# The MLP's two products as seven products of halves, with weight sums made by accumulating transfers

## The chip, the cores and the metric

One core of a Trainium2 chip runs the whole program. The time is device microseconds of one execution; lower is better. TensorE (PE) multiplies, VectorE (DVE), ScalarE (ACT) and GpSimd (POOL) work on tiles of 128 partitions in the on-chip memory SBUF, TensorE's sums lie in PSUM, and 16 DMA engines carry data between DRAM and SBUF. SyncE (SP) and POOL each have a queue that issues transfers; each engine works through its own instructions in order.

## The reference

One decoder layer in float32, 512 tokens of 2048 features: attention of 16 heads, then the part that is changed here.

```python
h = h + mix                                   # after the attention's output projection
h = h + squared_relu_mlp(rms_norm(h, norm_mlp_g[i]), mlp_w_in[i], mlp_w_out[i])

def squared_relu_mlp(h, w_in, w_out):         # w_in 2048 x 8192, w_out 8192 x 2048
    return jnp.square(jax.nn.relu(h @ w_in)) @ w_out
```

## The kernel before

Everything is held transposed: features on the partitions, the 512 tokens on the free axis. A float32 product is made of three: each operand is split into two float32r parts, `hi` (a rounded copy, made by ACT) and `lo` (the rest, made by DVE or POOL), and hi*hi + hi*lo + lo*hi go through TensorE into one PSUM bank. A weight block is 128 x 1024 (512 KB); SP loads it into `raw`, ACT casts it to `whi` (L101), DVE subtracts for `wlo` (L102). Each of these three names has 4 buffers.

The projections of q, k and v and the attention come first (L364 to L377) with heads staged between projection steps; then the output projection (`quad` on `wo`, L386 to L413). Its results are added to x into `y` (L419), and `hh`, `hl`, the two parts of y times the gain, and the sum of squares `acc2` (POOL, L430) are made on the way.

The MLP runs in 16 chunks of 512 hidden features. `mlp_in` multiplies a chunk of `w1` with `hh` and `hl` over 8 blocks (L140 to L142: weights stationary, 512 tokens moving); the token's RMS factor `rstd2` is made inside chunk 0 (L438 to L442) and applied to the products (L447), so that nothing waits for it. ACT squares and casts, DVE makes the rest (L449 to L451). `mlp_out` multiplies the chunk before with 8 blocks of `w2` (L463 to L465) and adds every bank into `y` (L467). The last chunk's sums are stored at once (L469). The order on each engine is set by a scheduler that follows the program's order and the buffers.

## Time and profile before

| | |
|---|---|
| runs | 2239.5 and 2240.43 us, median 2239.97 |
| profiled execution: span | 2237.2 us |
| instructions | 23734, of which 9866 matmuls and as many weight loads |
| PE / PEld / DVE / ACT / POOL busy | 99% / 82% / 47% / 32% / 13% |
| granted TensorE clock | full in every slice |
| moved by DMA | 215.46 MB, 96 GB/s over the span |

Of the profiled execution the span is given, from its first instruction to its last; the launch that surrounds it is only in the runs' times. A view of lines gives for each group of instructions the busy time, the mean of one, the idle time of its engine just before, and what ended most of that. PEld is the loading of the stationary side, shown as an engine of its own. Matmuls are pipelined, so one is shown as lasting longer than the distance between two starts.

### The profile page before, as it was taken

How to read it: one execution, taken by the hardware profiler on the slowest of the kernel's cores; microseconds unless marked ns; L12 is line 12 of the kernel's file. 1: busy time of each engine (PE TensorE's matmuls, PEld its weight loads, DVE VectorE, ACT ScalarE, POOL GpSimd, SP SyncE). 2: the span in 40 equal slices, each digit the busy share in tenths (PEclk: the TensorE clock that was granted, in tenths of full speed). 3: DMA queues.
4: the chain of work that ended last, by engine and by line, in shares of the span. 5: the costliest groups of instructions: out<-in, count | busy, mean ns of one | idle time of the engine just before them, and what ended most of it. 6: DMA issues, size and time to landing. Idle time of an engine off the chain costs nothing.

```text
span 2237.2 us, 23734 instructions
## 1 busy us (share of the span) xinstructions
PE 2213.0 (99%) x9866; PEld 1830.6 (82%) x9866; DVE 1053.6 (47%) x1178; ACT 723.8 (32%) x846; POOL 294.4 (13%) x150
## 2 busy tenths in 40 slices
PE   8999999999999999999999999999999999999999
PEld 7878878878888888888888888888888888888887
DVE  6574573673685334434334334344343343343343
ACT  5454454454464223212222222212222122222221
POOL 5444434434411111000000000000000000000000
PEclk9999999999999999999999999999999999999999
DMA  6222222222223333233332232332232323323323
GB/s 216 85 67 76 85 76 76 85 66 84 79 74 104 113 118 117 85 104 96 100 96 94 94 104 88 101 104 94 96 102 86 104 95 102 96 94 94 104 86 112
DMA packets 60443, 215.46 MB, mean 96 GB/s; under 512 B 6832, under 2 KB 6832, under 8 KB 60336
## 3 DMA queue, kind: packets, MB, share of 16 engines
q1 hardware_dynamic: 60336, 213.95, 29.8%
q8 instruction: 77, 1.26, 0.2%
q14 instruction: 30, 0.25, 0.0%
HBM read 209.73 MB, written 4.19 MB: 96 GB/s over the span
## 4 chain that ended last, share of the span: by engine, by line
PE 87%; DVE 8%; ACT 3%; POOL 1%; issue 1%; DMA 0%; SPq 0%; POOLq 0%; ACTq 0%; DVEq 0%
PE pm L141 13%; PE pm L140 13%; PE pm L142 13%; PE po L463 10%; PE po L465 10%; PE po L464 10%; PE pq L254 2%; PE pq L252 2%; PE pq L253 2%; PE pv L221 2%; PE pv L223 2%; PE pv L222 2%; DVE nb L115 1%; DVE sp L307 1%; DVE sp L304 1%
## 5 line engine op out<-in xcount | busy, mean ns | idle before, releaser
L101 ACT CAST whi<-raw 128x1024 fp32r<-128x1024 f32 (+1 forms) x385 | 405.2, 1052 | 1166.5 <-PE pm L141 566.0
L102 DVE TENSOR_TENSOR wlo<-raw,whi 128x1024 fp32r<-128x1024 f32 (+1 forms) x297 | 371.7, 1252 | 628.0 <-ACT whi L101 626.4
L140 PE MATMUL pm<-hh,whi 128*128 128x512 f32 x1024 | 398.7, 389 | 0.0
L142 PE MATMUL pm<-hh,wlo 128*128 128x512 f32 x1024 | 398.4, 389 | 0.0
L141 PE MATMUL pm<-hl,whi 128*128 128x512 f32 x1024 | 398.4, 389 | 0.0
L463 PE MATMUL po<-u,whi 128*128 128x512 f32 x1024 | 398.3, 389 | 0.0
L464 PE MATMUL po<-u,whi 128*128 128x512 f32 x1024 | 398.3, 389 | 0.0
L465 PE MATMUL po<-u,wlo 128*128 128x512 f32 x1024 | 398.3, 389 | 0.0
L467 DVE TENSOR_TENSOR y<-po,y 128x512 f32<-128x512 f32 x256 | 176.5, 689 | 248.4 <-PE po L465 247.7
L102 POOL TENSOR_TENSOR wlo<-raw,whi 128x1024 fp32r<-128x1024 f32 x88 | 224.3, 2549 | 303.0 <-ACT whi L101 303.0
L141 PEld LDWEIGHTS pm<-hl,whi 128*128 128x128 f32 x1024 | 192.3, 188 | 40.1 <-issue 0.2
L140 PEld LDWEIGHTS pm<-hh,whi 128*128 128x128 f32 x1024 | 192.3, 188 | 40.0 <-issue 0.2
L465 PEld LDWEIGHTS po<-u,wlo 128*128 128x128 f32 x1024 | 192.3, 188 | 39.9
L142 PEld LDWEIGHTS pm<-hh,wlo 128*128 128x128 f32 x1024 | 192.3, 188 | 39.9
L464 PEld LDWEIGHTS po<-u,whi 128*128 128x128 f32 x1024 | 192.3, 188 | 39.9
L463 PEld LDWEIGHTS po<-u,whi 128*128 128x128 f32 x1024 | 192.3, 188 | 39.8
L252 PE MATMUL pq<-xh,whi 128*128 128x512 f32 x512 | 200.1, 391 | 0.0
L254 PE MATMUL pq<-xh,wlo 128*128 128x512 f32 x512 | 199.4, 390 | 0.0
L253 PE MATMUL pq<-xl,whi 128*128 128x512 f32 x512 | 199.3, 389 | 0.0
L252 PEld LDWEIGHTS pq<-xh,whi 128*128 128x128 f32 x512 | 96.1, 188 | 20.5 <-ACT whi L101 0.2
L253 PEld LDWEIGHTS pq<-xl,whi 128*128 128x128 f32 x512 | 96.1, 188 | 20.5 <-issue 0.2
L254 PEld LDWEIGHTS pq<-xh,wlo 128*128 128x128 f32 x512 | 96.1, 188 | 20.4
(151 smaller groups left out, 2178.3 us busy)
## 6 DMA issues: line engine op xcount, KB each, us to landing
raw<-w SPq DMA_DIRECT2D x256, 512.0 KB, 3.5
raw<-wqk SPq DMA_DIRECT2D x64, 512.0 KB, 3.5
raw<-wo SPq DMA_DIRECT2D x32, 512.0 KB, 3.4
raw<-wv SPq DMA_DIRECT2D x31, 512.0 KB, 3.5
raw<-xT SPq DMA_DIRECT2D x15, 512.0 KB, 3.9
out<-y SPq DMA_DIRECT2D x16, 256.0 KB, 2.0
raw<-xT SPq DMA_DIRECT2D x2, 256.0 KB, 3.7
raw<-wv SPq DMA_DIRECT2D x2, 256.0 KB, 4.6
```

The lines of the kernel that those rows point to most:

```text
L101: nc.scalar.copy(hi, raw)
L102: lo_engine.tensor_tensor(lo, raw, hi.bitcast(F32), op=ALU.subtract)
L140: nc.tensor.matmul(pm[m], wh[:, ww], ah[k], start=k == 0, stop=False)
L141: nc.tensor.matmul(pm[m], wh[:, ww], al[k], start=False, stop=False)
L142: nc.tensor.matmul(pm[m], wl[:, ww], ah[k], start=False, stop=k == 2 * nb - 1)
L252: nc.tensor.matmul(pq, wh[:, ww], xh[k], start=k == 0, stop=False)
L253: nc.tensor.matmul(pq, wh[:, ww], xl[k], start=False, stop=False)
L254: nc.tensor.matmul(pq, wl[:, ww], xh[k], start=False, stop=k == KC - 1)
L463: nc.tensor.matmul(pm, wh[:, ww], uh[k], start=k == 0, stop=False)
L464: nc.tensor.matmul(pm, wh[:, ww], ul[k], start=False, stop=False)
L465: nc.tensor.matmul(pm, wl[:, ww], uh[k], start=False, stop=k == 3)
L467: nc.vector.tensor_tensor(ym, pm, ym, op=ALU.add)
```

## The change

The matrices of both MLP products are cut in halves in each direction, and each product of 2 x 2 halves is made by seven products instead of eight (one level of Strassen's scheme). With x11 to x22 the quarters of the left side and w11 to w22 those of the weights, products 1, 5, 6 and 4 take the weights w11, w11 + w12, w11 + w12 + w22 and w11 + w12 + w22 + w21 (signs lie on the other operand or in the adds), product 3 takes w22, 7 takes w12 + w22, 2 takes w21. They run in the order 1, 5, 6, 3, 7, 2, 4. The sums of weights are made by DMAs that POOL issues with `accum_op=ALU.add`: `plus` adds a block from DRAM onto a block in SBUF. w11 becomes in turn the four sums, in the same buffers.

The first product now runs in 16 units (`g`), each 7 products of 48 matmuls with 256 tokens moving; the second in 16 units (`s`, `fp`), each 7 products of 24 matmuls, with the hidden activations stationary and 512 output features moving, so that its result has tokens on the partitions. `y` is therefore transposed on TensorE after the output projection and written to DRAM (`yd`), and read back as `z` before the second product. The RMS factor is made before the first product and applied to `y` (`norm`), from which `make` forms the seven left operands in unit 0. The hidden activations' seven operands, in two parts, are written to DRAM for each unit of the first product (`put`: 14 pieces of 256 KB, POOL's queue) and read for each unit of the second (`fetch`, SP's queue). The part of the program up to the output projection is as it was, but for the pools that some constants come from.

```diff
-                nc.scalar.activation(hh[m], ym, AF.Copy, scale=g_sb[:, 1, m:m + 1])
-                nc.vector.scalar_tensor_tensor(
-                    hl[m], ym, g_sb[:, 1, m:m + 1], hh[m].bitcast(F32),
-                    op0=ALU.mult, op1=ALU.subtract,
-                )
...
+    pr = bank("pr")
+    nc.tensor.matmul(pr, ones_d, acc2, start=True, stop=True)
+    rstd2 = st("rstd2")
+    newton_rstd(st("r0"), st("nb"), pr, rstd2)
+    nc.vector.tensor_scalar(rstd2, rstd2, -0.5, None, op0=ALU.mult)
+    yd = dram.tile([P, KC * S], F32, name="yd")
+    def quarter(th, fp, fh):
+        return slice(((th * 2 + fp) * 2 + fh) * 1024, ((th * 2 + fp) * 2 + fh + 1) * 1024)
+    for c4 in range(4):
+        for t in range(4):
+            pt = pb.tile([P, S], F32, name="pt", tag="pb")
+            for i in range(4):
+                nc.tensor.transpose(
+                    pt[:, i * P:(i + 1) * P], y[:, 4 * c4 + i, t * P:(t + 1) * P], ident
+                )
+            ys = st("ys")
+            nc.scalar.copy(ys, pt)
+            q = quarter(t // 2, c4 // 2, c4 % 2).start + (t % 2) * S
+            nc.gpsimd.dma_start(yd[:, q:q + S], ys)
...
+    pp = ctx.enter_context(tc.tile_pool(name="pp", bufs=4, space=PSUM))
+    def banks(name):
+        return pp.tile([P, 1024], F32, name=name, tag="pp")
+    def operand(r, i, part):
+        name = f"x{r}{part}{i}"
+        if r in (1, 2, 4):
+            return mp.tile([P, S], F32R, name=name, tag=name)
+        k = 4 * {5: 0, 6: 1, 7: 2, 3: 3}[r] + i
+        return big.tile([P, S], F32R, name=name, tag=f"a{part}{k}")
+    def products(src):
+        def chunk(i, j, pool, tag):
+            ts = [pool.tile([P, 1024], F32, name=tag, tag=tag, bufs=4) for _ in range(2)]
+            for c in range(2):
+                nc.sync.dma_start(ts[c], src[i, j, c])
+            return ts
+        def plus(ts, i, j):
+            for c in range(2):
+                nc.gpsimd.dma_start(ts[c], src[i, j, c], accum_op=ALU.add)
+        w11 = chunk(0, 0, wpool, "raw")
+        w22 = chunk(1, 1, mp, "mraw")
+        w12 = chunk(0, 1, mp, "mraw")
+        plus(w12, 1, 1)
+        w21 = chunk(1, 0, wpool, "raw")
+        into = {1: w11, 5: w11, 6: w11, 4: w11, 3: w22, 7: w12, 2: w21}
+        then = {1: (0, 1), 5: (1, 1), 6: (1, 0)}
+        for r in ORDER:
+            parts = []
+            for c in range(2):
+                w = into[r][c]
+                hi, lo = wtile("whi"), wtile("wlo")
+                split_w(hi, lo, w, nc.vector)
+                parts.append((hi, lo))
+            if r in then:
+                plus(w11, *then[r])
+            yield r, parts
...
+    def split(r, i, src):
+        hi, lo = operand(r, i, "hi"), operand(r, i, "lo")
+        nc.scalar.copy(hi.rearrange("p (o c) -> p o c", o=2), src)
+        nc.vector.tensor_tensor(
+            lo.rearrange("p (o c) -> p o c", o=2), src,
+            hi.rearrange("p (o c) -> p o c", o=2).bitcast(F32), op=ALU.subtract,
+        )
+        xs[r, i] = hi, lo
+    def block(t, k, i):
+        return y[:, 8 * k + 2 * i:8 * k + 2 * i + 2, 256 * t:256 * (t + 1)]
+    def norm(k):
+        for c in range(8 * k, 8 * k + 8):
+            nc.vector.scalar_tensor_tensor(
+                y[:, c, :], y[:, c, :], g_sb[:, 1, c:c + 1], rstd2, op0=ALU.mult, op1=ALU.mult
+            )
+    def make(r):
+        tt = nc.vector.tensor_tensor
+        if r == 1:
+            norm(0)
+        for i in range(4):
+            x11, x12, x21, x22 = (block(t, k, i) for t in range(2) for k in range(2))
+            if r == 1:
+                split(1, i, x11)
+            elif r == 5:
+                split(4, i, x22)
+                tt(x22, x21, x22, op=ALU.subtract)
+                split(5, i, x22)
+            elif r == 6:
+                tt(x21, x11, x21, op=ALU.subtract)
+                tt(x11, x22, x11, op=ALU.subtract)
+                split(6, i, x11)
+            elif r == 3:
+                split(2, i, x12)
+                tt(x12, x12, x11, op=ALU.add)
+                split(3, i, x12)
+            elif r == 7:
+                split(7, i, x21)
+    ud = [dram.tile([P, 14 * S], F32R, name=f"ud{g}") for g in range(NG)]
+    for g in range(NG):
+        ps, kept = {}, {}
+        for r, parts in products(w1[g]):
+            if g == 0:
+                make(r)
+            b = {1: "A", 2: "A", 6: "B", 7: "B", 4: "B", 5: "C", 3: "C"}[r]
+            new = b not in ps
+            if new:
+                ps[b] = banks(f"p{b}")[:, :S]
+            for c, (wh, wl) in enumerate(parts):
+                for kk in range(4):
+                    k = 4 * c + kk
+                    h, l = (x[:, (k % 2) * 256:(k % 2 + 1) * 256] for x in xs[r, k // 2])
+                    for m in range(2):
+                        ww = slice(kk * 256 + m * P, kk * 256 + (m + 1) * P)
+                        o = ps[b][:, m * 256:(m + 1) * 256]
+                        kw = dict(stop=False, skip_group_check=True)
+                        nc.tensor.matmul(o, wh[:, ww], h, start=new and k == 0 and m == 0, **kw)
+                        nc.tensor.matmul(o, wh[:, ww], l, start=False, **kw)
+                        nc.tensor.matmul(o, wl[:, ww], h, start=False, stop=k == 7,
+                                         skip_group_check=True)
+            tt = nc.vector.tensor_tensor
+            if r == 1:
+                p1 = kept[2, 1] = st("p1")
+                nc.scalar.copy(p1, ps["A"])
+            elif r == 5:
+                q = kept[2, 2] = st("q")
+                tt(q, ps["C"], p1, op=ALU.subtract)
+            elif r == 6:
...
+            elif r == 2:
+                u = kept[1, 1] = st("u")
+                nc.scalar.activation(u, ps["A"], AF.Relu)
+                nc.scalar.activation(u, u, AF.Square)
+            else:
+                tt(p1, ps["B"], p1, op=ALU.add)
+            if r in (3, 7, 4):
+                u = {3: v, 7: q, 4: p1}[r]
+                nc.scalar.activation(u, u, AF.Relu)
+                nc.scalar.activation(u, u, AF.Square)
+        if spill is None:
+            spill = big.tile([P, KC, S], F32R, name="spill", tag="acc")
+        def put(r, u):
+            hi, lo = spill[:, r - 1, :], spill[:, 7 + r - 1, :]
+            nc.scalar.copy(hi, u)
+            nc.vector.tensor_tensor(lo, u, hi.bitcast(F32), op=ALU.subtract)
+            for n in (r - 1, 7 + r - 1):
+                nc.gpsimd.dma_start(
+                    ud[g][:, n * S:(n + 1) * S].bitcast(F32), spill[:, n, :].bitcast(F32)
+        u11, u12, u21, u22 = (kept[t, f] for t in (1, 2) for f in (1, 2))
+        put(1, u11)
+        put(4, u22)
+        tt(u22, u21, u22, op=ALU.subtract)
+        put(5, u22)
+        tt(u21, u11, u21, op=ALU.subtract)
+        put(7, u21)
+        tt(u11, u22, u11, op=ALU.subtract)
+        put(6, u11)
+        put(2, u12)
+        tt(u12, u12, u11, op=ALU.add)
+        put(3, u12)
+    z = big.tile([P, KC * S], F32, name="z", tag="acc")
+    for h in range(2):
+        nc.sync.dma_start(z[:, h * 4096:(h + 1) * 4096], yd[:, h * 4096:(h + 1) * 4096])
+    e1 = [[st("e1") for _ in range(2)] for _ in range(2)]
+    NS = NG // 2
+    def fetch(s):
+        for r in ORDER:
+            for j in range(2):
+                i = 2 * (s % 2) + j
+                pair = operand(r, i, "hi"), operand(r, i, "lo")
+                for n, x in enumerate(pair):
+                    k = 7 * n + r - 1
+                    nc.sync.dma_start(
+                        x.bitcast(F32), ud[2 * s + j][:, k * S:(k + 1) * S].bitcast(F32)
+                    )
+                xs[r, i] = pair
+    fetch(0)
+    for s in range(NS):
+        for fp in range(2):
+            if fp and s < NS - 1:
+                fetch(s + 1)
+            for r, parts in products(w2[s, fp]):
+                b = {1: "A", 2: "A", 6: "B", 7: "B", 4: "B", 5: "C", 3: "C"}[r]
+                new = b not in ps
+                if new:
+                    ps[b] = banks(f"p{b}")
+                for c, (wh, wl) in enumerate(parts):
+                    h, l = xs[r, 2 * (s % 2) + c]
+                    for kk in range(2):
+                        for t in range(2):
+                            tt = slice(kk * 256 + t * P, kk * 256 + (t + 1) * P)
+                            nc.tensor.matmul(o, h[:, tt], wh[:, ww], start=k0, stop=False,
+                                             skip_group_check=True)
+                            nc.tensor.matmul(o, h[:, tt], wl[:, ww], start=False, stop=False,
+                                             skip_group_check=True)
+                            nc.tensor.matmul(o, l[:, tt], wh[:, ww], start=False,
+                                             stop=c == 1 and kk == 1, skip_group_check=True)
...
+                if r == 1:
+                    for t in range(2):
+                        e, pt = e1[fp][t], ps["A"][:, t * S:(t + 1) * S]
+                        if s == 0:
+                            nc.scalar.copy(e, pt)
+                        else:
+                            tt(e, pt, e, op=ALU.add)
...
+                elif r == 5:
+                    tt(zq[2, 2], ps["C"], zq[2, 2], op=ALU.add)
+                elif r == 6:
+                    tt(zq[1, 2], zq[1, 2], ps["B"], op=ALU.subtract)
+                elif r == 3:
+                    tt(zq[1, 2], ps["C"], zq[1, 2], op=ALU.add)
+                elif r == 7:
+                    tt(zq[2, 2], zq[2, 2], ps["B"], op=ALU.subtract)
+                elif r == 2:
+                    tt(zq[1, 1], ps["A"], zq[1, 1], op=ALU.add)
+                else:
+                    tt(zq[2, 1], ps["B"], zq[2, 1], op=ALU.add)
...
```

Line numbers in the three pieces of order below are those of the kernel they come from; `whi`, `wlo`, `raw` and `u` are as above, `mraw` are four more block buffers for w22 and w12, `spill` holds what goes to DRAM, `ud` is that DRAM, and a number behind a name tells one tile from another.

ACT in the kernel before, between two chunks: the casts of weight blocks, and the activations of the hidden features when a chunk's banks are done.

```order
L101 CAST whi_8230<-raw_8228 128x1024
L101 CAST whi_8292<-raw_8290 128x1024
L449 ACTIVATE scratch_6089<-scratch_6088 128x512
L450 CAST u_6072<-scratch_6089 128x512
L449 ACTIVATE scratch_6091<-scratch_6090 128x512
L449 ACTIVATE scratch_6093<-scratch_6092 128x512
...
L450 CAST u_6075<-scratch_6095 128x512
L101 CAST whi_8360<-raw_8358 128x1024
L101 CAST whi_8366<-raw_8364 128x1024
```

Every cast there reads a block of its own. ACT in the changed kernel, from product 1 of one unit to its product 7: the first three pairs of casts read the same two blocks.

```order
L108 CAST whi_10085<-raw_10067 128x1024
L108 CAST whi_10089<-raw_10068 128x1024
...
L108 CAST whi_10146<-raw_10067 128x1024
L108 CAST whi_10150<-raw_10068 128x1024
L597 ACTIVATE p1_9675<-p1_9675 128x512
L598 ACTIVATE p1_9675<-p1_9675 128x512
L605 CAST spill_6751<-q_9736 128x512
L108 CAST whi_10207<-raw_10067 128x1024
...
L108 CAST whi_10211<-raw_10068 128x1024
...
L108 CAST whi_10268<-mraw_10071 128x1024
L108 CAST whi_10272<-mraw_10072 128x1024
L108 CAST whi_10327<-mraw_10075 128x1024
```

Behind the third pair stand the casts of products 3 and 7 from other buffers. POOL, which before had only the adds of L430 in this part of the program and nothing after them, has in the changed kernel for the same unit:

```order
L486 DMA mraw_10075<-w1 128x1024
L486 DMA mraw_10076<-w1 128x1024
L608 DMA ud7_6161<-spill_6751 128x512 x4
L486 DMA raw_10067<-w1 128x1024
L486 DMA raw_10068<-w1 128x1024
L608 DMA ud7_6161<-spill_6751 128x512 x2
L486 DMA raw_10067<-w1 128x1024
L486 DMA raw_10068<-w1 128x1024
L608 DMA ud7_6161<-spill_6751 128x512 x7
L486 DMA raw_10067<-w1 128x1024
L608 DMA ud7_6161<-spill_6751 128x512
L486 DMA raw_10068<-w1 128x1024
```

The three pairs onto `raw_10067` and `raw_10068` are the sums for products 5, 6 and 4; the stores between them carry the activations of the unit before.

## Rows read from the trace of the kernel before

**Rows 1.** Page, span and part 1: busy us, share of span, instructions.
```profile
PE 2213.0 (99%) x9866; PEld 1830.6 (82%) x9866; DVE 1053.6 (47%) x1178; ACT 723.8 (32%) x846; POOL 294.4 (13%) x150
```
**Rows 2.** Page, part 4: the chain that ended last, by engine and line.
```profile
PE 87%; DVE 8%; ACT 3%; POOL 1%; issue 1%; DMA 0%; SPq 0%; POOLq 0%; ACTq 0%; DVEq 0%
PE pm L141 13%; PE pm L140 13%; PE pm L142 13%; PE po L463 10%; PE po L465 10%; PE po L464 10%; PE pq L254 2%; PE pq L252 2%; PE pq L253 2%; PE pv L221 2%; PE pv L223 2%; PE pv L222 2%; DVE nb L115 1%; DVE sp L307 1%; DVE sp L304 1%
```
**Rows 3.** Timeline, PE around 839.7 us: start us, us, instruction.
```profile
839.70 0.39 PE L140 MATMUL pm<-hh,whi 128*128 128x512 f32 x1
```
**Rows 4.** Timeline, the end of the span, PE and DVE.
```profile
2233.02 0.39 PE L465 MATMUL po<-u,wlo 128*128 128x512 f32 x1
2233.44 0.69 DVE L467 TENSOR_TENSOR y<-po,y 128x512 f32<-128x512 f32 x1 [2.03 <-PE po L465]
```
**Rows 5.** Busy time in one stretch, the MLP; last granted clock, DMA share, GB/s.
```profile
839.70:2233.00 1393.30, 1393.30 (x6146) 1153.72 (x6145) 566.84 (x646) 341.04 (x390) 6.63 (x4) 1.00 0.31 98
```
**Rows 6.** Waits, 850 to 2237 us: us in total, times, longest.
```profile
DVE wlo L102 <- ACT whi L101: 548.6, 173, 4.2
ACT whi L101 <- PE po L464: 495.0, 124, 8.5
ACT whi L101 <- PE pm L141: 480.1, 111, 4.4
```
**Rows 7.** Timeline, a head's last product, PE and its weight loads.
```profile
703.09 0.28 PE L345 MATMUL po<-ah,vh 128*128 128x256 f32 x1
703.09 0.19 PEld L346 LDWEIGHTS po<-al,vh 128*128 128x128 f32 x1
703.21 0.28 PE L346 MATMUL po<-al,vh 128*128 128x256 f32 x1
703.21 0.19 PEld L347 LDWEIGHTS po<-ah,vl 128*128 128x128 f32 x1
703.33 0.28 PE L347 MATMUL po<-ah,vl 128*128 128x256 f32 x1
...
703.45 0.38 PE L348 MATMUL po<-a,v 128*128 128x128 f32 x2
...
703.59 0.47 PE L140 MATMUL pm<-oh,whi 128*128 128x512 f32 x1
```
**Rows 8.** Timelines of POOL, PE and DVE around the RMS factor.
```profile
839.98 6.86 POOL L430 TENSOR_TENSOR acc<-acc,sq 128x512 f32<-128x512 f32 x4 [36.65 <-ACT sq L429]
...
853.30 1.02 PE L440 MATMUL pr<-acc,ones_d 128*128 128x512 f32 x2
...
858.00 0.43 DVE L442 TENSOR_SCALAR rstd<-rstd 128x512 f32<-128x512 f32 x1
```
**Rows 9.** Groups by line and shape: busy us, mean ns | idle before.
```profile
L102 DVE TENSOR_TENSOR wlo<-raw,whi 128x1024 fp32r<-128x1024 f32 x295 | 370.3, 1256 | 626.8 <-ACT whi L101 625.1
...
L467 DVE TENSOR_TENSOR y<-po,y 128x512 f32<-128x512 f32 x256 | 176.5, 689 | 248.4 <-PE po L465 247.7
...
L101 ACT CAST whi<-raw 128x1024 fp32r<-128x1024 f32 x383 | 403.9, 1055 | 1166.0 <-PE pm L141 566.0 <-PE po L464 495.0 <-PE pq L253 45.6
...
L450 ACT CAST u<-scratch 128x512 fp32r<-128x512 f32 x64 | 37.9, 617 | 0.5
...
L430 POOL TENSOR_TENSOR acc<-acc,sq 128x512 f32<-128x512 f32 x15 | 24.5, 1631 | 133.7 <-ACT sq L429 132.9
```
**Rows 10.** DMA: queue totals; then issues: count, KB each, median us to landing.
```profile
q1 hardware_dynamic: 60336, 213.95, 29.8%
...
raw<-w SPq DMA_DIRECT2D x256, 512.0 KB, 3.5
...
out<-y SPq DMA_DIRECT2D x16, 256.0 KB, 2.0
```
**Rows 11.** Busy time in one early stretch; columns as in rows 5.
```profile
40.00:50.00 10.00, 10.00 (x46) 8.28 (x45) 5.82 (x2) 3.70 (x4) 8.26 (x4) 1.00 0.59 211
```
**Rows 12.** Page, part 5: one group of weight loads.
```profile
L141 PEld LDWEIGHTS pm<-hl,whi 128*128 128x128 f32 x1024 | 192.3, 188 | 40.1 <-issue 0.2
```

More of the change, by code (lines that the diff above doesn't have):

```diff
@@ L69, in trunk @@
     )
-    ntri_r = const.tile([P, P], F32R, name="ntri_r")
+    ntri_r = ap.tile([P, P], F32R, name="ntri_r")
     nc.vector.tensor_copy(ntri_r, ntri)
@@ L77, in trunk @@
     )
-    keep = const.tile([P, P], F32, name="keep")
+    keep = ap.tile([P, P], F32, name="keep")
     nc.vector.memset(keep, 1.0)
-    cap = const.tile([P, P], F32, name="cap")
+    cap = ap.tile([P, P], F32, name="cap")
     nc.vector.memset(cap, 0.0)
@@ L396, in trunk, with st @@
     mp = ctx.enter_context(tc.tile_pool(name="mlp", bufs=1))
-    pb = ctx.enter_context(tc.tile_pool(name="pb", bufs=4, space=PSUM))
-    def tmp2(name, n):
-        t = mp.tile([P, S], F32, name=name, tag="tmp2", bufs=2)
-        return t[:, :n]
-    hh = [mp.tile([P, S], F32R, name="hh", tag=f"hh{k}") for k in range(KC)]
-    hl = [mp.tile([P, S], F32R, name="hl", tag=f"hl{k}") for k in range(KC)]
-    acc2 = mp.tile([P, S], F32, name="acc2")
-    rstd2 = mp.tile([P, S], F32, name="rstd2")
+    pb = first_psum.enter_context(tc.tile_pool(name="pb", bufs=4, space=PSUM))
+    def st(name):
+        return mp.tile([P, S], F32, name=name, tag="st", bufs=6)
     y = big.tile([P, KC, S], F32, name="y", tag="acc")
+    acc2 = st("acc2")
     for mq in range(4):
@@ L427, in trunk @@
                 else:
-                    sq = tmp2("sq2", S)
+                    sq = st("sq2")
                     nc.scalar.activation(sq, ym, AF.Square)
                     nc.gpsimd.tensor_tensor(acc2, acc2, sq, op=ALU.add)
-    u_all = chunks("u", "ahi")
-    scratch = chunks("scratch", "alo", 8, F32)
-    def mlp_in(c):
-        for step, pm in enumerate(quad(w1[c], 8, hh, hl)):
-            if c == 0 and step == 4:
-                pr = pb.tile([P, S], F32, name="pr", tag="pb")
-                nc.tensor.matmul(pr, ones_d, acc2, start=True, stop=True)
-                newton_rstd(tmp2("r0", S), tmp2("nb", S), pr, rstd2)
-                nc.vector.tensor_scalar(rstd2, rstd2, -0.5, None, op0=ALU.mult)
-        i = 8 * (c % 2)
-        uh, ul = u_all[i:i + 4], u_all[i + 4:i + 8]
-        for m in range(4):
-            r = scratch[2 * m]
-            nc.vector.scalar_tensor_tensor(r, pm[m], 0.0, rstd2, op0=ALU.max, op1=ALU.mult)
-            u = scratch[2 * m + 1]
-            nc.scalar.activation(u, r, AF.Square)
-            nc.scalar.copy(uh[m], u)
-            nc.vector.tensor_tensor(ul[m], u, uh[m].bitcast(F32), op=ALU.subtract)
-        return uh, ul
@@ L454, in mlp_out @@
-    def mlp_out(c, u):
-        uh, ul = u
-        for mq in range(4):
-            w = [weights(w2[c, mq, b], nc.vector) for b in range(2)]
-            for m in range(4):
-                pm = pb.tile([P, S], F32, name="po2", tag="pb")
-                for k in range(4):
-                    wh, wl = w[k // 2]
-                    ww = slice((k % 2) * S + m * P, (k % 2) * S + (m + 1) * P)
-                    nc.tensor.matmul(pm, wh[:, ww], uh[k], start=k == 0, stop=False)
-                    nc.tensor.matmul(pm, wh[:, ww], ul[k], start=False, stop=False)
-                    nc.tensor.matmul(pm, wl[:, ww], uh[k], start=False, stop=k == 3)
-                ym = y[:, 4 * mq + m, :]
-                nc.vector.tensor_tensor(ym, pm, ym, op=ALU.add)
-                if c == NCH - 1:
-                    nc.sync.dma_start(out[:, (4 * mq + m) * S:(4 * mq + m + 1) * S], ym)
@@ L471, in trunk @@
-    u = mlp_in(0)
-    for c in range(1, NCH):
-        un = mlp_in(c)
-        mlp_out(c - 1, u)
-        u = un
-    mlp_out(NCH - 1, u)
+    pr = bank("pr")
[6 more added lines that the diff above has]
+        return slice(((th * 2 + fp) * 2 + fh) * 1024, ((th * 2 + fp) * 2 + fh + 1) * 1024)
```

59 lines of the change are left out of this document (45 added, 14 removed).

## The prediction

> **What bounds the kernel now.** I read the page's first part and its chain before anything else. TensorE is busy 99% of the span and carries 87% of the chain that ended last, most of it on the MLP lines L140 to L142 and L463 to L465 [rows 1, 2]. The reader is to see that no other engine is near: VectorE 47%, ScalarE 32%, GpSimd 13%. Then I cut out the MLP by its first and last matmul: the first with `hh` starts at 839.70, and the last one starts at 2233.02 and is followed by one VectorE add [rows 3, 4]. The stretch between them has 6146 matmuls, TensorE never idle, granted clock 1.00, DMA share 0.31 at 98 GB/s [rows 5]. So 62% of the span is a plain stream of matmuls, and its price is one pitch: 1393.3 us for the 6144 MLP matmuls is 0.2268 us for each of 512 columns. Fewer matmuls pay in full, as long as operands come in time. The waits say how much in time they are: ScalarE's weight casts wait for buffers that TensorE still holds, 495.0 us and 480.1 us in total, and VectorE waits for ScalarE [rows 6]. The side engines run on slack, and so do the transfers.
>
> The sum is made against the span of 2237.2 us. The two runs, 2239.5 and 2240.43 us, lie 2.3 and 3.2 us above it, so I start from 2240.
>
> **Products on TensorE.** The new loops (7 products, 2 blocks, 4 slices, 2 halves, 3 parts) give each of 16 units of the first product 336 matmuls with 256 columns moving, 5376 in all; with 2 slices of 512 columns each of 16 units of the second has 168, 2688 in all. Each had 3072 of 512. For 256 columns the attention has rows: three in a row start 0.12 us apart [rows 7]. First product: 5376 x 0.12 = 645 us for 697, -52. Second: 2688 x 0.2268 = 610 us for 697, -87. Together **-139 us**.
>
> **The new head of the MLP.** Before, the RMS chain lay inside chunk 0. Now the sum of squares, the factor, the scaling of `y` and the first split stand between the output projection and the first product. GpSimd's four adds ended at 846.84; from the `pr` matmul to the finished factor it was 853.30 to 858.43, or 5.1 us [rows 8]. Then eight scalings at 0.69, a cast at 0.62 and a subtraction at 0.69 [rows 9] bring the first product to about 859 instead of 839.7: +19 us. The 64 transposes lie inside this gap: 64 x 0.14 us by the 128-column rows (703.45 to 703.59, [rows 7]) is 9 us, and their 16 copies and stores go three at a time (16 x (0.62 + 2.0) / 3 = 14 us, [rows 9, 10]). Without that cover they would add 5 to 15 us. Unit 0 also makes all `x` operands on VectorE: 52 more tile operations at 0.69 are 36 us beside its regular 29, against 40 us of matmuls, so +20. The join of the two products and the larger last store I take as +3. Sum **+42**.
>
> **Splits and combinations.** A unit now splits 14 blocks. VectorE per unit of the first product: 14 x 1.256 + 16 x 0.689 = 28.6 us, ScalarE 14 x 1.055 + 16 x 0.62 = 24.7 us [rows 9], against 336 x 0.12 = 40.3 us on TensorE; in the second product VectorE has about 26.5 us against 168 x 0.2268 = 38.1. Cost nothing, covered by TensorE. GpSimd issues 22 transfers in such a unit. No row has one issued there; at the 1.63 us of its own small add [rows 9] that is 36 us, still beside the 38 to 40 of TensorE. I take nothing.
>
> **The transfers.** Here the change is large. A unit loads 8 blocks of 512 KB as before, adds 8 more onto them, and writes (or later reads) 14 pieces of 256 KB. Price of a plain transfer: the page gives 213.95 MB in 29.8% of the span, 321 GB/s while the engines are busy; the best stretch, 40 to 50 us, 211 GB/s at share 0.59, 357 GB/s [rows 10, 11]. I take 357, since the queues will be fuller than ever: 1.47 us for 512 KB, 0.73 for 256 KB; 321 (1.63 us) goes into the range. An accumulating transfer appears nowhere. From below it costs what a plain block costs, 1.47; from above a read of the source, a read of the target and a write, each as long as a transfer, 3 x 1.47. I take **twice**, because a plain copy reads and writes side by side, and what is added is one more read of the same length. The Trainium skill (Collectives: The Full Stack, the section on the bandwidth ceiling and the fold count) says that a sum made in the DMA engines needs two source reads on the same ring and so ran at about half of a copy, 1.93 measured; no run here shows it yet, and by its figure the sum would be some 26 us lower.
>
> Unit: 8 x 1.47 + 8 x 2.94 + 14 x 0.73 = 45.5 us of all 16 engines. That is more than TensorE's 40.3 and 38.1. So the transfers become the bound: 16 x 5.2 + 16 x 7.4 = **+201 us**.
>
> **Sum:** 2240 - 139 + 42 + 201 = about **2345 us**.
>
> **Why the wait cannot be hidden.** The same block is summed in place three times, and products 1, 5 and 6 follow each other directly. Between two of them lie: a sum lands, ScalarE casts (1.055), VectorE subtracts (1.256), GpSimd issues the next sum onto the block, it lands. Landing takes 3.5 us for a plain block [rows 10], so 5.0 with a second read: 7.3 us per link against 5.76 us of matmuls (5.44 in the second product). A late sum stops ScalarE's in-order queue, and behind it stand the casts of products 3 and 7, whose blocks have long been there, and the activations of the products before. That is the low end of this case: were the engines never full, two links per unit would cost 16 x 2 x (1.5 + 1.9) = 109 us, 2252. The high end is the page's 321 GB/s: units of 50.5 us, +361, 2505. **This case: 2250 to 2505, chance 0.50.**
>
> **Rivals.**
> - *The sums are as cheap as loads; faster than before.* If the second read hides in the first, a unit needs 33.7 us of transfers, under TensorE's 38.1, and a link takes 2.3 + 3.5 = 5.8 us against 5.76 and 5.44: 16 x 2 x (0.05 + 0.37) = 13 us. 2240 - 139 + 42 + 13 = **2156**, range 2140 to 2195. For it: DMA stands at a share of 0.31 in the MLP [rows 5], and blocks land 3.5 us after their issue at any load. Against it: target data must be read from somewhere. It decides as soon as a sum costs less than 1.3 plain blocks. Chance 0.22.
> - *In between, a sum at 1.5 blocks.* Units of 39.6 us of transfers, links of 6.5 us: 16 x 2 x (0.8 + 1.1) = 61, **2204**. Within 2%. Chance 0.17.
> - *Three passes.* Units of 57.3 us: 16 x 17.0 + 16 x 19.2 = 579, **2722**. For it only that no row excludes it. Chance 0.08.
> - *Weight loads bind.* A load of the stationary side is shown as 188 ns [rows 12], and with 256 columns there is one load for each 107 ns of columns at 2.4 GHz, the granted level. If a load held its path for 188 ns, the first product would take 5376 x 0.188 = 1011 us, 366 more than above. Those units (63 us) would cover their transfers, and the second product would keep its 118: 2143 + 366 + 118 = **2627**. Against it: in [rows 7] three loads shown at 0.19 each start 0.12 apart, so they overlap. Chance 0.03. The Trainium skill (Trainium Kernel Development and Optimization, Best Practices) tells to judge the distance from the limit by the busy share of the weight loads and not of the matmuls; by that rule 82% [rows 1] leaves little room for a load per 256 columns, and the trace's overlapping loads speak against reading it so here.
>
> **Chances and range.** The predicted time is that of the likeliest case, 2345. About 2% is what a measurement tells from no change: 2195 to 2285 us. Slower by more: the first case without its low corner (0.47), three passes, bound loads, and a little of the middle: 0.59. Within: 0.18. Faster: 0.23, nearly all from cheap sums. The range of 8 in 10 runs from 2150 to 2510; it leaves out the two dear rivals (0.11) and the lower part of the cheap one.
>
> **What would show each step.** (1) TensorE's starts in the first product 0.12 us apart inside a product of 48; 0.19 would prove the loads. (2) DMA share near 0.9 or more through the MLP, instead of 0.31; a share of 0.6 or less with a fast run would prove cheap sums. (3) The median from issue to landing of the accumulating blocks: over 5 us for this case, 3.5 for the cheap rival. (4) TensorE idle in every unit before products 5 and 6, released by ScalarE's cast of the in-place block, which itself waited for the sum; none before 3, 7, 2 and 4. (5) A hole of about 19 us before the first product and some 20 us more in unit 0. (6) The time of the stretch up to 839 us unchanged.
> Wrong I would be above all in the price of a sum: each tenth of a block moves the time by about 38 us once the engines are full.

## The result, and the profile after

The changed kernel takes **2384.92 us** (median of 2380.51 and 2389.33) against 2239.97: 1.065 times as long, 95% interval 1.0628 to 1.0671. The forecast was 2345 us, slower, with 2250 to 2505 for the likeliest case. The profiled execution has a span of 2378.8 us.

Below, from the page: the first part, the DMA line of its 40 slices (busy share in tenths), its two queues, and its issues with the median us from issue to landing. They answer to [rows 1, 10].

```profile
PE 2186.2 (92%) x11850; PEld 1886.1 (79%) x11850; DVE 1342.6 (56%) x1422; ACT 1005.8 (42%) x1198; POOL 648.9 (27%) x646
...
DMA  6222222222234358999999999999999999999885
...
q0 software_dynamic: 56064, 197.16, 38.0%
q1 hardware_dynamic: 91728, 276.88, 32.4%
...
raw<-w POOLq DMA_DIRECT2D x192, 512.0 KB, 6.6
...
mraw<-w POOLq DMA_DIRECT2D x64, 512.0 KB, 9.1
```

TensorE, 99% busy before, is now 92% busy, and the transfer engines are at nine tenths through the MLP. The six blocks of a unit that are summed onto `raw` (three sums of two blocks, for products 5, 6 and 4) land after 6.6 us, the two for product 7 after 9.1, where a plain block took 3.5 before.

The same by stretch (us, busy us of PE, PEld, DVE, ACT, POOL with their instructions, granted clock, DMA share, GB/s), answering to [rows 5]. The first row ends where the old MLP began.

```profile
0.00:839.00 839.00, 819.54 (x3714) 677.19 (x3715) 467.71 (x518) 373.21 (x443) 289.84 (x151) 1.00 0.31 97
839.00:870.00 31.00, 19.97 (x110) 16.24 (x109) 23.28 (x34) 20.52 (x37) 15.47 (x21) 0.78 0.67 204
...
1000.00:1500.00 500.00, 460.18 (x3622) 450.15 (x3622) 292.55 (x324) 251.70 (x321) 161.34 (x239) 0.97 0.95 260
...
1700.00:2100.00 400.00, 361.90 (x1478) 286.21 (x1477) 218.31 (x193) 128.64 (x126) 60.30 (x70) 0.95 0.97 268
```

What TensorE waits for from 880 us on (us in total, times, longest); product 5 works in `pC`, products 6, 7 and 4 in `pB`, L571 and L573 belong to the first product of the MLP, L664 and L666 to the second:

```profile
PE pC L664 <- ACT whi L108: 29.9, 10, 9.9
PE pB L666 <- DVE wlo L109: 20.7, 23, 2.9
PE pC L571 <- ACT whi L108: 20.3, 13, 3.4
PE pB L664 <- ACT whi L108: 18.3, 15, 2.2
PE pB L664 <- issue: 15.2, 1, 15.2
PE pB L571 <- ACT whi L108: 12.4, 11, 2.1
PE pB L573 <- DVE wlo L109: 12.2, 19, 0.8
PE pC L573 <- DVE wlo L109: 10.8, 16, 0.8
PE pC L666 <- DVE wlo L109: 8.0, 13, 0.8
```

Together 147.8 us. All but the 15.2 us (one gap, at the join of the two products) is a wait, ahead of product 5 or 6, for the split of the block that is summed in place: its cast waits for a transfer. Here is one unit of the first product, on ScalarE, VectorE, GpSimd and TensorE (start us, us, instruction, idle time before it). From 1230.82 on the casts are, in pairs, for products 1, 5 and 6:

```profile
1230.82 1.05 ACT L108 CAST whi<-raw 128x1024 fp32r<-128x1024 f32 x1
1233.70 1.05 ACT L108 CAST whi<-raw 128x1024 fp32r<-128x1024 f32 x1 [1.83 <-PE pA L572]
...
1244.49 1.05 ACT L108 CAST whi<-raw 128x1024 fp32r<-128x1024 f32 x1 [7.92 <-DMA raw<-w]
1247.10 1.05 ACT L108 CAST whi<-raw 128x1024 fp32r<-128x1024 f32 x1 [1.56 <-DMA raw<-w]
...
1252.94 1.04 ACT L108 CAST whi<-raw 128x1024 fp32r<-128x1024 f32 x1 [2.21 <-DMA raw<-w]
...
1255.68 1.05 ACT L108 CAST whi<-raw 128x1024 fp32r<-128x1024 f32 x1 [0.66 <-DMA raw<-w]
...
1231.90 1.23 DVE L109 TENSOR_TENSOR wlo<-raw,whi 128x1024 fp32r<-128x1024 f32 x1 [0.34 <-ACT whi L108]
...
1227.58 0.89 POOL L486 DMA_DIRECT2D mraw<-w  x1 [12.60 <-DVE wlo L109]
1228.81 0.85 POOL L486 DMA_DIRECT2D mraw<-w  x1 [0.34 <-DVE q L588]
...
1239.10 1.81 POOL L486 DMA_DIRECT2D raw<-w  x2 [3.28 <-issue]
1240.45 1.60 POOL L608 DMA_DIRECT2D ud<-spill  x2
1247.22 0.91 POOL L486 DMA_DIRECT2D raw<-w  x1 [5.18 <-DMA raw<-w]
1249.81 0.88 POOL L486 DMA_DIRECT2D raw<-w  x1 [1.68 <-DVE wlo L109]
...
1239.38 0.28 PE L571 MATMUL pA<-x1hi,whi 128*128 128x256 f32 x1
...
1245.59 0.39 PE L571 MATMUL pC<-x5hi,whi 128*128 128x256 f32 x1 [0.28 <-ACT whi L108]
...
1246.85 0.39 PE L573 MATMUL pC<-x5hi,wlo 128*128 128x256 f32 x1 [0.76 <-DVE wlo L109]
```

The link from product 1's cast to product 5's is 13.67 us for the first half of the block (1230.82 to 1244.49) and 13.40 for the second; from 5 to 6 it is 8.45 and 8.58. TensorE needs 5.76 us for a product. The first link contains a piece that I had not priced: the subtract ends at 1233.13, but its sum is issued at 1239.10. GpSimd's queue is in order. The sum for product 7 (`mraw<-w`) stands ahead of it, after 12.60 us of waiting, then come stores, and GpSimd waits 3.28 us for something that the trace does not name. After the issue, 5.4 us pass until the cast. Not all of a link is lost, for the casts run ahead of TensorE: product 1's stands 8.6 us before TensorE begins that product (1239.38), so of the 13.67 us only 0.28 and 0.76 us are left as waits ahead of product 5.

### The profile page after: what moved, and what is told of

Its sections match the earlier page's. It is cut to its first block, busy times and chain, and to the rows that moved or that the text cites. A ratio compares the mean times of both kernels' runs of the same rounds, so it can differ in the third digit from the quotient of the medians.

```text
span 2378.8 us, 30383 instructions
## 1 busy us (share of the span) xinstructions
PE 2186.2 (92%) x11850; PEld 1886.1 (79%) x11850; DVE 1342.6 (56%) x1422; ACT 1005.8 (42%) x1198; POOL 648.9 (27%) x646
## 3 DMA queue, kind: packets, MB, share of 16 engines
q1 hardware_dynamic: 91728, 276.88, 32.4%
## 5 line engine op out<-in xcount | busy, mean ns | idle before, releaser
L109 DVE TENSOR_TENSOR wlo<-raw,whi 128x1024 fp32r<-128x1024 f32 (+1 forms) x361 | 445.3, 1234 | 646.9 <-ACT whi L108 643.9
L486 POOL DMA_DIRECT2D raw<-w x192 | 172.7, 913 | 648.8 <-DVE wlo L109 448.0
L109 POOL TENSOR_TENSOR wlo<-raw,whi 128x1024 fp32r<-128x1024 f32 x88 | 223.2, 2537 | 305.8 <-ACT whi L108 305.8
L608 POOL DMA_DIRECT2D ud<-spill x224 | 138.6, 662 | 138.4 <-ACT spill L605 64.8
L486 POOL DMA_DIRECT2D mraw<-w x64 | 55.6, 869 | 390.6 <-DMA mraw<-w 137.0
L109 DVE TENSOR_TENSOR wlo<-mraw,whi 128x1024 fp32r<-128x1024 f32 x128 | 153.2, 1218 | 4.1 <-ACT whi L108 2.6
L108 ACT CAST whi<-mraw 128x1024 fp32r<-128x1024 f32 x128 | 128.3, 1047 | 50.2 <-PE pB L668 30.7
L147 PE MATMUL pm<-oh,whi 128*128 128x512 f32 x256 | 99.8, 390 | 0.0
L148 PE MATMUL pm<-ol,whi 128*128 128x512 f32 x256 | 99.7, 389 | 0.0
L149 PE MATMUL pm<-oh,wlo 128*128 128x512 f32 x256 | 99.6, 390 | 0.0
L571 PE MATMUL pC<-x5hi,whi 128*128 128x256 f32 x256 | 78.9, 308 | 20.3 <-ACT whi L108 20.3
L571 PE MATMUL pB<-x6hi,whi 128*128 128x256 f32 x256 | 79.4, 310 | 14.2 <-ACT whi L108 12.4
L573 PE MATMUL pB<-x6hi,wlo 128*128 128x256 f32 x256 | 80.5, 314 | 12.4 <-DVE wlo L109 12.2
L573 PE MATMUL pC<-x5hi,wlo 128*128 128x256 f32 x256 | 79.1, 309 | 10.8 <-DVE wlo L109 10.8
L226 PE MATMUL pv<-whi,xh 128*128 128x512 f32 x208 | 82.5, 397 | 5.7 <-DVE qk L261 5.7
```

The lines of the kernel that those rows point to most:

```text
L108: nc.scalar.copy(hi, raw)
L109: lo_engine.tensor_tensor(lo, raw, hi.bitcast(F32), op=ALU.subtract)
L147: nc.tensor.matmul(pm[m], wh[:, ww], ah[k], start=k == 0, stop=False)
L148: nc.tensor.matmul(pm[m], wh[:, ww], al[k], start=False, stop=False)
L149: nc.tensor.matmul(pm[m], wl[:, ww], ah[k], start=False, stop=k == 2 * nb - 1)
L486: nc.gpsimd.dma_start(ts[c], src[i, j, c], accum_op=ALU.add)
```

## The experiments

Three theories. **A**, the prediction's: the transfer engines are full and set the unit. **B**: the link (split, issue, landing) between products 1, 5 and 6 sets it, and the engines are merely busy. **C**, formed after the eighth run: both limits lie close together. The unit of the first product is read from ScalarE's copy `p<-pA`, one a unit, that of the second from VectorE's `z<-pC,z`; first and last start, divided by 15. The changed kernel's rows (ns least/median/most; first and last start):

```profile
L578 ACT COPY p<-pA x16: 573/578/580, 872.6 to 1586.9; 128x512 f32<-128x512 f32 x16
L684 DVE TENSOR_TENSOR z<-pC,z x16: 1212/1217/1225, 1672.8 to 2348.7; 128x1024 f32<-128x1024 f32 x16
```

All runs, read in the same way; the ratios are to the kernel before, timed beside them (2239.97 to 2240.59 us). Share and landing are the transfer engines' in 1000:1500 and the median of the sums onto the first tile.

| kernel | us | ratio, 95% interval | unit 1st / 2nd, us | share | landing, us |
|---|---|---|---|---|---|
| changed | 2384.92 | 1.0628 to 1.0671 | 47.6 / 45.1 | 0.95 | 6.6 |
| e1_copy | 2190.10 | 0.9762 to 0.9791 | 41.4 / 39.2 | 0.85 | 5.1 |
| e2_apart | 2353.62 | 1.0460 to 1.0522 | 47.0 / 43.2 | 0.97 | 7.7 |
| e3_mix | 2170.69 | 0.9679 to 0.9708 | 41.0 / 37.7 | 0.84 | 6.6 |
| e4_dve | 2166.05 | 0.9656 to 0.9685 | 41.1 / 38.0 | 0.58 | none |
| e5_half | 2395.48 | 1.0669 to 1.0707 | 49.3 / 44.9 | 0.82 | 6.6 |
| e6_link | 2247.74 | 1.0023 to 1.0049 | 42.6 / 41.2 | 0.93 | 8.2 |
| e7_sbuf | 2429.99 | 1.0836 to 1.0870 | 50.1 / 44.9 | 0.90 | 6.5 |
| e8_zlate | 2164.77 | 0.9650 to 0.9681 | 41.1 / 38.3 | 0.57 | none |
| e9_late | 2355.90 | 1.0502 to 1.0533 | 46.8 / 44.8 | 0.87 | 6.8 |
| e10_both | 2296.30 | 1.0238 to 1.0273 | 45.6 / 41.2 | 0.89 | 7.7 |
| e11_load | 2227.32 | 0.9931 to 0.9946 | 41.4 / 40.3 | 1.02 | 8.9 |
| e12_fewer | 2247.76 | 1.0012 to 1.0047 | 43.8 / 41.0 | 0.87 | 5.9 |

**e1_copy: copies in place of sums.**

```
-  nc.gpsimd.dma_start(ts[c], src[i, j, c], accum_op=ALU.add)
+  nc.gpsimd.dma_start(ts[c], src[i, j, c])
```

> The eight sums of a unit become eight plain copies onto the same tiles, at the same place, on the same queue and behind the same waits; the weights are then not summed, so the output is not the reference's. Theory A (the transfer engines are full, a sum costs two blocks): a unit has 16 blocks of 1.47 us and 14 stores or fetches of 0.73 us, 33.7 us, under TensorE's 40.3 and 38.1; the time falls to 2140 to 2200 us, and the share of the transfer engines to about 0.8. Theory B (a sum's way from the subtract to its landing, on the link between products 1, 5 and 6, sets the unit, and its 6.6 to 9.1 us are latency that a copy has too): 2300 to 2390 us.

2190.10 us. What a sum takes beyond a copy is what costs; but a copy is also issued in 0.54 us against 0.88 and lands in 5.1 against 6.6, so the link got shorter too. Against B's numbers, for A's, and no proof of A.

**e2_apart: one other product between any two sums.**

```
+ APART = (1, 2, 5, 3, 6, 7, 4)     # before: (1, 5, 6, 3, 7, 2, 4)
```

> The same bytes in the same operations, but the products run in the order 1, 2, 5, 3, 6, 7, 4, so that each sum onto the first tile has one whole other product (5.76 or 5.44 us) more before it is needed. Theory A (transfer engines full): nothing is saved, 2360 to 2410 us. Theory B (the link sets the unit): the link has 11.5 us for 1.055 + 1.256 + 0.9 + 6.6 = 9.8 us, so most of the waits ahead of products 5 and 6 go, 2150 to 2230 us.

2353.62 us, just under A's band. It is not as clean as I meant it. The waits ahead of product 5 did not all go, the largest line of all is one in the second product; and products that share an accumulator now follow each other, so that TensorE waits for it to be read (same columns as above):

```profile
PE pC L672 <- ACT whi L109: 33.4, 8, 9.0
PE pA L572 <- ACT p L579: 25.7, 13, 3.9
PE pC L672 <- DVE z L692: 17.7, 1, 17.7
PE pB L572 <- DVE v L585: 16.2, 15, 2.7
```

**e3_mix and e4_dve: sums on VectorE.**

```
+  def add(ts, us):
+      for c in range(2):
+          nc.vector.tensor_tensor(ts[c], ts[c], us[c], op=ALU.add)
-  plus(w12, 1, 1)                   # ahead of the products
-  if r in then: plus(w11, *then[r])
+  if r == 1:   add(w11, w12); plus(w12, 1, 1)   # e4: add(w12, w22)
+  elif r == 5: add(w11, w22)
+  elif r == 6: plus(w11, 1, 0)                  # e4: add(w11, w21)
```

> The two sums on the link (for products 5 and 6) are made by VectorE from blocks that are in SBUF anyway, the other two stay sums by transfers. Transfers of a unit: 8 x 1.47 + 4 x 2.94 + 14 x 0.73 = 33.7 us; VectorE gets 4 adds of 1.256 us, 28.6 + 5.0 = 33.6 and 26.5 + 5.0 = 31.5 us, under TensorE's 40.3 and 38.1. Theories A and B both expect 2140 to 2200 us, since this takes away the load and the link; a theory that TensorE itself is slower in the changed kernel than 0.12 and 0.227 us a product expects over 2250.

> All four sums of a unit are made by VectorE, none by a transfer: 8 adds of 1.256 us more, 38.6 us of VectorE in a unit of the first product and 36.5 in the second, against TensorE's 40.3 and 38.1; transfers 22 us. Theories A and B: 2140 to 2230 us, by how far a VectorE that is busy 96% of a unit keeps up. If VectorE's row has to queue behind the joins and splits, over 2230 and TensorE's waits name VectorE instead of a transfer.

2170.69 and 2166.05 us: both are faster than the kernel before as well, by 3.1% and 3.3%. In e3 TensorE waits over 2 us only at the join:

```profile
PE pB L671 <- issue: 26.2, 1, 26.2
```

Its row for 880 to 1500 us shows what the seven products cost when nothing holds them up (columns as in the stretches above):

```profile
880.00:1500.00 620.00, 614.23 (x5101) 612.62 (x5102) 494.29 (x541) 369.23 (x463) 168.18 (x270) 1.00 0.83 246
```

**e5_half: only the sum for product 7 on VectorE.** It is e3's `add`, called as `add(w12, w22)` when r is 5, with the three sums onto `w11` left as they were.

> One of the four sums of a unit, the one for product 7 that no link waits for, is made by VectorE; the three sums onto the first tile, with the links between products 1, 5, 6 and 4, stay transfers. Transfers of a unit fall from 45.5 to 8 x 1.47 + 6 x 2.94 + 14 x 0.73 = 39.6 us, just under TensorE's 40.3 in the first product and just over its 38.1 in the second. Theory A (full transfer engines): 2190 to 2270 us. Theory B (the link sets the unit): the link is untouched, 2350 to 2390 us.

2395.48 us at a share of 0.82: A's band is missed by 125 us, B's by 5. But the edit also brought a wait of its own. The scheduler moved the add of the next unit up VectorE's queue, where it waits for a load, with the running unit's joins and the split of product 2 behind it; in the first product TensorE waits 28.8 us in total for that split (`PE pA L578 <- DVE wlo L109`):

```profile
1283.70 1.23 DVE L490 TENSOR_TENSOR mraw<-mraw 128x1024 f32<-128x1024 f32 x1 [8.25 <-DMA mraw<-w]
```

**e6_link: only the sum for product 5 on VectorE.** Again e3's `add(w11, w12)` when r is 1, and the other three sums are transfers; the one for product 7 is now issued behind it.

> One of the four sums of a unit, this time the one on the link from product 1 to product 5, is made by VectorE (subtract 1.256 and add 1.256 us in place of a transfer that landed after 6.6 us); the other three stay transfers. The same 39.6 us of transfers as when the sum for product 7 is made by VectorE. Theory A: the two agree within 30 us, 2190 to 2270 us. Theory B: the waits ahead of product 5 go and those ahead of product 6 stay, 2270 to 2330 us, and well under the other.

2247.74 us, in A's band with the transfers of e5, but 148 us away from e5. Equal bytes, unequal times: A alone cannot be it. B's band (2270 to 2330) is missed by 22 us, but TensorE's waits ahead of product 5 are gone, as B said, and those ahead of product 6 remain:

```profile
PE pB L670 <- ACT whi L108: 21.5, 8, 7.3
PE pB L670 <- issue: 19.8, 1, 19.8
PE pB L672 <- DVE wlo L109: 17.2, 17, 4.1
```

**e7_sbuf: sums by transfers from the block already in SBUF.** It is e4 with `nc.gpsimd.dma_start(ts[c], us[c], accum_op=ALU.add)` in `add`.

> All four sums stay accumulating transfers, but their source is the block that is in SBUF already and not DRAM; DRAM is read 8 blocks fewer a unit. If the DMA engines' own time per summed block is what is full (theory A), 2330 to 2410 us, as with sums from DRAM. If reading DRAM is what is full, the transfers from DRAM fall to 22 us a unit and the time to 2170 to 2230 us.

2429.99 us, slightly above the band. Reading DRAM is not what is scarce: a sum costs the engines as much from SBUF. Software queue 36.9% of 2428.0 us, less 164.6 us for its 240 stores (7.6% of e4's span, where it has only them), by 256 sums is 2.86 us; from DRAM it was 2.89. The order on GpSimd differs too: here the sum for product 7 is issued behind the one for product 5. Hardly a wait ahead of product 5 is left, but those ahead of product 6 are more than twice as long as in the changed kernel:

```profile
PE pB L578 <- ACT whi L108: 74.6, 30, 7.3
PE pB L671 <- ACT whi L108: 56.6, 18, 6.0
```

**e8_zlate: e4 with the residual behind the operands.**

```
-  for h in range(2): nc.sync.dma_start(z[:, h * 4096:(h + 1) * 4096], yd[:, h * 4096:(h + 1) * 4096])
   ...
   fetch(0)
+  for fp in range(2):
+      for a, b in ((1, 1), (0, 1), (0, 0), (1, 0)):
+          q = quarter(a, fp, b)
+          nc.sync.dma_start(z[:, q], yd[:, q])
```

> All sums on VectorE (2166.05 us in the run before), and between the two products the 28 blocks of operands (0.25 MB each) are fetched ahead of the residual (4 MB, which now comes behind them in quarters) instead of behind it. In the run before TensorE stood 14.5 us before product 7 of the second product's first unit. If it stood for the operands behind the residual (4 MB at 1.47 us for 0.5 MB, 11.8 us), 2152 to 2160 us; if for anything else, 2164 to 2168 us; if VectorE's joins now wait for the residual and hold the accumulators, over 2168 us.

2164.77 us: nothing won, and the premise was wrong. SyncE's queue in e4, at the join, shows the residual (`z`) issued behind 25 of the 28 operands already:

```profile
1537.92 0.32 SPq L646 DMA_DIRECT2D x4hi<-ud  x1
1547.08 0.79 SPq L635 DMA_DIRECT2D z<-yd  x2
...
1549.51 0.95 SPq L481 DMA_DIRECT2D mraw<-w  x2
```

The last three operands and the next weight blocks stand behind it. Probably the queue stands there until the residual's buffer is free; that was not tried. A gap of 5 to 29 us at the join stays in all kernels.

**e9_late and e10_both.** e9 makes the last sum in place, for product 4, on VectorE; there nothing of the links 1, 5, 6 is touched and no load is waited for. e10 is e9 with the order of e2.

```
-  if r in then: plus(w11, *then[r])
+  if r == 6: add(w11, w21)
+  elif r in then: plus(w11, *then[r])
```

> The sum for product 4, the last on the first tile, is made by VectorE right behind the splits of product 6, where VectorE waits for no load; the sums for products 5, 6 and 7 stay transfers, and the order of products stays. Transfers 39.6 us a unit. Where VectorE made the sum for product 7, the time was 2395.48 us, but VectorE stood 8.25 us there in front of its add for a block still in transfer, with the splits behind it. Theory A (full transfer engines alone): 2190 to 2270 us. Theory B (the links 1, 5, 6 alone, untouched here): 2350 to 2390 us. Theory C (two limits close to each other, the transfers and the links; both must go): 2280 to 2370 us, with waits ahead of products 5 and 6 and transfer engines that are no longer full.

> The two half measures together: the order 1, 2, 5, 3, 6, 7, 4, which alone gave 2353.62 us, and the sum for product 4 on VectorE, 39.6 us of transfers a unit. Theory A: the same as with the second half alone, within 30 us. Theory B: the same as with the first half alone, 2330 to 2360 us. Theory C: both limits are relieved, 2180 to 2250 us.

2355.90 and 2296.30 us. The first lies in B's band and in C's. e9 has the bytes of e6 and is 108 us slower, with engines at 0.87 and no wait of its own on VectorE: cleaner evidence against A alone than e5, though e6 also issues the sum for product 7 later. e10 lies between all bands, under both halves but 46 us above C's; it pays e2's accumulator waits again (in its waits `PE pB L578 <- DVE v L591` leads with 24.4 us).

**e11_load and e12_fewer: each limit by itself.** e11 is e3 with dummy traffic in place of the saved sums, e12 the changed kernel with fewer stores and fetches.

```
e11: def add(ts, us): ...
+        for n in range(2): nc.gpsimd.dma_start(bal, us[c])     # bal: its own place in DRAM each time
e12:
-  for n in (r - 1, 7 + r - 1):
+  for n in (r - 1, 7 + r - 1) if g < 4 else ():
-  if fp and s < NS - 1: fetch(s + 1)
+  if fp and s < 1: fetch(s + 1)
```

> Full transfer engines without the links: the sums for products 5 and 6 are made by VectorE as in the kernel that took 2170.69 us, and in place of the four summing transfers saved in a unit, eight plain transfers of 0.5 MB (a block in SBUF to a place in DRAM that nobody reads) are issued on GpSimd's queue: 33.7 + 8 x 1.47 = 45.4 us of transfers a unit, as in the changed kernel. Theory A (full transfer engines alone set the unit): 2330 to 2400 us. Theory B (the links alone): 2165 to 2210 us. Theory C (two limits, the later one counts): 2290 to 2380 us, with the transfer engines at 0.95 or more.

> The links without full transfer engines: all four sums of a unit stay transfers in the order of the changed kernel; left out are the stores of the operands after the first four units of the first product and their fetches after the second step of the second, whose products go on with old operands, so the output is not the reference's. Transfers of most units: 45.5 - 14 x 0.73 = 35.2 us. Theory A: TensorE's time again, 2170 to 2220 us. Theory B: 2350 to 2390 us. Theory C: the links stay and a sum lands somewhat earlier, 2260 to 2340 us, with the waits ahead of products 5 and 6 and the transfer engines under 0.85.

2227.32 and 2247.76 us. Both fall between the bands: e11 17 us over B's and 63 under C's, e12 28 over A's and 12 under C's. As they were stated, A is refuted by the first, B by the second, and C sized both limits too dear. The stretches of e11 (columns as above) show engines fuller than in the changed kernel. TensorE has nearly no gaps in the first product; in the second it waits ahead of product 1, whose block is a plain load (last line, columns of the waits):

```profile
1000.00:1500.00 500.00, 498.84 (x4153) 498.19 (x4152) 388.19 (x423) 288.89 (x370) 190.01 (x317) 1.00 1.02 347
1650.00:2000.00 350.00, 332.20 (x1406) 269.42 (x1407) 253.09 (x225) 125.05 (x121) 66.05 (x100) 0.97 1.03 347
...
PE pA L677 <- ACT whi L108: 26.6, 10, 9.8
```

Against e3's 2170.69, full engines without links cost 57 us, links with 0.87 of the engines 77, and both together (the changed kernel) 214. That is 80 us more than the sum of the two, so in these runs each makes the other dearer. What fits this, but is not shown: with the links in place, fuller engines land the sums later (6.6 us against 5.9), and every such delay stands on the link; with no links, e11's landings of 8.9 us (the sum for product 4) hold up little. But e12 also takes the stores off GpSimd's queue in 12 of the 16 units of the first product, and they stood among its sums; and e3 and e11 issue the sum for product 7 later than the other two. How much of the 80 us is landing and how much is GpSimd's queue, the runs do not separate.

## Why the prediction was right in sign and near in size, and not for its reason

**Products on TensorE, -139: right.** Starts lie 0.12 us apart, as product 4 of a unit shows:

```profile
1003.06 0.28 PE L572 MATMUL pB<-x4lo,whi 128*128 128x256 f32 x1
1003.18 0.28 PE L573 MATMUL pB<-x4hi,wlo 128*128 128x256 f32 x1
1003.30 0.28 PE L571 MATMUL pB<-x4hi,whi 128*128 128x256 f32 x1
```

In e3 the copy `p<-pA` stands at 924.11 in unit 1 and at 1488.6 in unit 15: 40.3 us a unit, the 40.3 forecast; the second product's 37.7 answers to 38.1. So the rival of weight loads that bind at 0.188 us is refuted. The loads are 98.8% busy in e3's row above (612.62 of 620 us) and the 0.12 us hold all the same.

**New head, +42: 10 us short, and its parts are off both ways.** The first product starts at 864.20 instead of 839.70, so +24.5 and not +19. Unit 0 takes TensorE 52.8 us (its next unit starts at 916.98), +12.5 over the 40.3 and not +20. The join is the term mis-sized: 3 us taken, 15.2 us of gap. Together 52 us; in e3 it is 25.6 + 11.2 + 26.2 = 63 us. e3 has these two terms and little else: 2170.69 against 2240 - 139 + 42 = 2143, and 21 of the 28 us between are this term. Up to 839 us nothing changed, as said.

**Price of a sum, twice a plain block: right.** (38.0% of 2378.8 us - 164.6 us) / 256 = 2.89 us. A plain block took 1.46 us in the same run (32.4% of the span for 276.88 MB), and as a copy at the same place 1.58 (e1: 26.0% of 2189.5 us, less 164.6, by 256). That is 1.8 to 2.0 blocks. The Trainium skill (Collectives: The Full Stack, the section on the bandwidth ceiling and the fold count) gives 1.93 as the measured ratio between a collective that copies and one that sums with two source reads; the 1.8 to 2.0 here agree with it. The cheap rival, the one at 1.5 and the three passes fall.

**The transfers, +201: this step failed, though its number came out.** That the forecast came within 40 us is luck for this term: e11, with engines at least as full and no links, stands 57 us over e3 and not 201. I made it "the transfers become the bound" and took 45.5 us a unit. Units measured 47.6 and 45.1 us, and share times unit is 0.95 x 47.6 = 45.2 and 0.97 x 45.1 = 43.7 us of full engines: the load was sized well. But it does not set the time. In e11 1.02 x 41.4 = 42.2 us of load a unit passed in 41.4. By e11's share of 1.03, the changed kernel's load alone would need units of 43.9 and 42.4 us; over e3's 41.0 and 37.7 that is 16 x (2.9 + 4.7) = 122 us, an estimate that ends near 2290 and not at 2385. And where the load fell by 6 us a unit without touching the links (e9), 29 us came back instead of the 177 that the step claims (201 - 16 x 1.5).

**"Why the wait cannot be hidden": the mechanism that I put at the low end is needed for the rest.** I had counted it only for engines that are never full; with full ones both act, and neither alone makes the 214 us. I had the link at 7.3 us: landing 5.0, and an issue that costs nothing. Measured were 8.45 to 13.67 in the unit shown. Landing is 6.6 us, not 5.0. The load is about a microsecond of that: in the changed kernel the first three sums onto `raw`, issued from 826.82 to 837.76 while the engines' share was 0.40 to 0.74, landed after 5.3 to 5.4 us. Nor does landing follow the share closely: it is 6.6 to 6.8 in e3, e5 and e9 at 0.82 to 0.87, and 5.9 in e12 at 0.87. The Trainium skill (DMA: Bandwidth & Descriptors, the section on queues, rings and completion order) says that an engine takes turns between the queues it has work for, by which a sum would share its time with the loads of the other queue; that a plain `w` block landed 3.5 us after issue before and lands on SyncE's queue after 8.0 now fits that, and the prediction's "at any load" does not hold. The issue is 0.88 us of GpSimd, and its in-order queue adds up to 6 us in the unit shown. With 1.05 + 1.23 + 0.88 + 6.6 = 9.8 us a link, and two links a unit, 40.3 + 2 x (9.8 - 5.76) = 48.4 and 38.1 + 2 x (9.8 - 5.44) = 46.8: within 1.7 us of the units measured. That is partly luck, and no model: the sum leaves out how far the casts run ahead, and with e12's 5.9 us it gives 47.0 and 45.4 where 43.8 and 41.0 were measured. I costed GpSimd's 22 issues at nothing since they fit beside TensorE; that they stand on the link, and in which order, I did not ask.

The waits also cost clock. Behind some of them the granted clock fell to the lower of its two levels (0.50 from 1211 to 1213, after TensorE had stood ahead of product 6 at 1207); behind those at 1245 and 1254 it stayed full. 20 us stretches with such a fall mostly show 0.83 or 0.91. The mean is 0.964, and 0.989 in e3, where TensorE stood only at the head and the join. By an estimate from these means, 2378.8 x 0.036 - 2169.1 x 0.011 = 62 us is the most this can be, since a slow clock costs nothing while TensorE waits. With 147.8 us of waits against 26.2 it makes up at most 183 of the 214 us; the rest stays open.

**The signs named.** (1) 0.12 us and (2) a share over 0.9 came as forecast; (3) landing over 5 us also; (4) the waits stand before products 5 and 6, and hardly elsewhere; (5) the hole was 24.5 us, and unit 0 added less than forecast; (6) as said. So all but the sizes in (5) came, but none of them could tell full engines from the links. A kernel with the same load and no links, or the reverse, does.

**Left open.** Which part of the first link GpSimd's order makes. In the changed kernel the sum for product 7 is issued ahead of those for products 5 and 6, which are needed earlier, and from 880 us on GpSimd stands still ahead of it for 268 us in total, for a split or a load alone (`POOL mraw L486`, 134.5 and 133.5 us). In e3, e6 and e11, all fast, it comes behind; e9 and e12 keep it ahead. But the order is not the whole: e1 keeps it ahead and is fast at 2190 us, and e7 issues it behind the sum for product 5 and is the slowest at 2430, with the waits moved from product 5 to product 6. To issue it later and change nothing else was not run.

## What to carry to other kernels

When a change loads a shared resource and puts its operations in series as well, price both: the busy time of the resource, and the chain of issue, landing and dependent steps with the landing as it is *under that load*, not as it is in the idle kernel. Here full engines without the chain cost 57 us (e11 against e3), and a chain of copies that land after 5.1 us only 19 (e1 against e3), while both together cost 214. And where the addend is in SBUF anyway, an add on an engine with slack (e3, e4: 5 to 10 us of VectorE a unit) can beat a transfer that costs the computing engines only its issue: here 2166 us against 2385, and against 2240 without the seven products.

## What the hardware showed that I had not expected

- GpSimd takes 0.88 us to issue a summing transfer of 512 KB (e3), 0.54 us for a copy of the same block (e1), and 0.54 to 0.59 for a store of 256 KB (e4, e3).
- A sum from SBUF costs the transfer engines what a sum from DRAM costs: 2.86 us (e7) and 2.89 us a block (the changed kernel).
- The engines ran at 347 GB/s where most transfers were plain (e11, two sums a unit) and at 260 GB/s with four sums a unit (the changed kernel), at shares of 1.02 and 0.95.
